# The four x tiles issued by ScalarE's queue at the start of a two-layer encoder kernel

## The chip, the core and the metric

The kernel runs on one core of one Trainium2 chip. The metric is the device time of one execution in microseconds (us). The engines are TensorE (PE, with PEld for its weight loads), VectorE (DVE), ScalarE (ACT), GpSimd (POOL) and SyncE (SP), which only issues DMAs here.

## The reference

x is 512 x 1024, float32. There are two layers. Each computes a modulation from the vector c, normalises x, projects it through a wide `w_in`, runs three token mixers, gates them and projects back:

```python
c_act = jax.nn.silu(c)
for l in range(DEPTH):
    mod = c_act @ w_ada[l] + b_ada[l]
    shift, scale, gate = [m[:, None, :] for m in split_cols(mod, (D, D, D))]
    h = rms_norm(x, g_pre[l]) * (1.0 + scale) + shift
    (cq, ckv, kr, za, qb_, kb_, vb_, zb, qc, kc, vc, zc, gcols) = split_cols(h @ w_in[l], IN_SPLITS)
    o_a = (mla_branch(cq, ckv, kr, ...) * jax.nn.silu(za)) @ w_o_mla[l]
    o_b = (swa_branch(qb_, kb_, vb_, ...) * jax.nn.silu(zb)) @ w_o_swa[l]
    o_c = (diff_branch(qc, kc, vc, ...) * jax.nn.silu(zc)) @ w_o_diff[l]
    y = (g[:, :, 0] * o_a + g[:, :, 1] * o_b + g[:, :, 2] * o_c) @ w_out[l]
    x = x + gate * rms_norm(y, g_post[l])
```

## The kernel before

Every matrix product in full precision is made of three matmuls (`mm3`, L86 to L89): each operand is split into a rounded part, made by ACT (`act_copy`, L81), and a rest, made by DVE or POOL (`sub`, L84). Tokens lie in the free dimension, 512 wide; the model dimension is cut into eight tiles of 128, numbered j = 0 to 7 here.

The change lies in the first stage, `layer0_input` and what is written ahead of it. It does these things:

- c is loaded (L156) and put through its silu: a tanh on ACT (L180) and two small steps on DVE (L181, L182) make `cact`.
- The modulation's shift and scale for layer 0 are a product of `cact` and `w_ada`. `mod_load` (L143) loads column tiles of `w_ada` on SP's queue, `mod_chunk` (L187) multiplies them on DVE, one 128-row slice after the other (L203 for the first slice, L206 for the rest), adds up the partitions with tiny matmuls (L212) and leaves shift and scale in `ashf` and `amul` (L215, L217, L220). There are chunks for j = 0, for 1, for 2 and 3, for 4 and 5, and for 6 and 7. The tiles of chunk 0 are called wh and wl, later ones wh, wl and big.
- x is loaded in four token tiles of 128 x 1024 (`xt0`, called big, L165 and L166). `normed` (L322) takes each through a square and sum on ACT (L325), an addition on DVE (L318), a power on POOL (L319) and a scaling on DVE (L327). PE transposes the result (L346), ACT copies it out (L349 by way of L81).
- Then for each j ACT applies scale and shift (L363) and makes the rounded part of h (called hTh, L81), DVE the rest (hTl, L84). Two products follow on PE: the mixer's inputs (`mla_in_step`, weights called u and p, into ps_sc, ps_sc, ps_pj and ps_av, 416 columns) and three column tiles of z (weights loaded to tf, split into pt by ACT and POOL, into ps_dn, ps_dn and ps_tr, 512 columns; L369 to L371, nine matmuls for each j).
- The small parameters of `setup_small` come last: four loads for each lambda (L412), products and sums on DVE (L415, L417), an exponential on ACT (L418).
- After the stage ACT takes the statistics of the mixer's inputs (L612, L614), and the attention of the first mixer begins.

The code does not fix the order on an engine. A scheduler puts the instructions in order with a time model of its own, engine by engine; the order it leaves is static, and each engine works through its list. So an edit in one place can move instructions in others. A load signals its end on one of eight semaphores, which the loads of SP's and ACT's queues take in turn: a load waits until the one that had its semaphore eight loads earlier has landed. Buffers of one name are used in rotation.

Of the kernel before, what the change touches and what calls it, by code (L numbers as in the profile page):

```python
# [17 lines left out]
P = 128  # L18
# [3 lines left out]
NT = S // P  # L22
# [28 lines left out]
def hybrid_kernel(ctx, tc, x, c, w_ada, b_ada, g_pre, g_post, w_in, g_q, w_uq, g_kv, w_ukv,  # L51
# [6 lines left out]
    pe, act, dve, pool, sp = nc.tensor, nc.scalar, nc.vector, nc.gpsimd, nc.sync  # L58
# [4 lines left out]
    def T(tag, shape, dt=F32, bufs=None):  # L63
        count[0] += 1
        return sb.tile(shape, dt, tag=tag, name=f"{tag}_{count[0]}",
                       bufs=bufs or BUFS.get(tag, 1))
# [76 lines left out]
    def mod_load(l, j, n, tags):  # L143
        tags = iter(tags)
        res = []
        for which in range(2):
            raws = [T(next(tags), [P, KT // n, n * P]) for _ in range(n)]
            for i, raw in enumerate(raws):
                loads.append(sp.dma_start(out=raw, in_=w_ada[l].rearrange("(p k) b -> p k b", k=KT)
                             [:, i * (KT // n):(i + 1) * (KT // n),  # L150
                              which * D + j * P:which * D + (j + n) * P]))
            res.append([raws[k * n // KT][:, k % (KT // n)] for k in range(KT)])
        return res

    xt0 = [T("big", [P, D]) for _ in range(NT)]
    sp.dma_start(out=cT, in_=c.rearrange("b (p k) -> p (b k)", k=KT))  # L156
    src0 = mod_load(0, 0, 1, ("wh", "wl"))
    prm = [T("tf", [P, P]) for _ in range(2)]
# [2 lines left out]
    for k, src, n in ((PR_GQ, g_q, 2), (PR_GKV, g_kv, 1), (PR_GSUB, g_sub, 1)):  # L161
        pool.dma_start(out=prm[1][k - 32:k - 32 + n * DEPTH, :],
                       in_=src.rearrange("l (a b) -> (l a) b", b=P))
    pool.dma_start(out=prm[1][0:16, :], in_=b_ada[1, 0:2 * D].rearrange("(a b) -> a b", b=P))
    for t in range(NT):  # L165
        sp.dma_start(out=xt0[t], in_=x[t * P:(t + 1) * P, :])  # L166
    prT = []

    for i, n in enumerate((32, PR_ROWS - 32)):
# [1050 lines left out]
```

## Time and profile before

| | us |
|---|---|
| median of 3 runs | 1180.55 (1180.5 to 1180.76) |
| profiled execution | 1178.78 |
| span of its instructions | 1176.7 |
| PE busy | 1146.0 (97%) |
| DVE busy | 844.2 (72%) |
| ACT busy | 631.5 (54%) |
| POOL busy | 181.3 (15%) |

The span runs from the first to the last instruction of the profiled execution; its own time is 2.1 us more. Busy times are sums over the whole kernel, so what one stage is bound by has to be read from windows and from the timeline of that stage.

### The profile page before, as it was taken

How to read it: one execution, taken by the hardware profiler on the slowest of the kernel's cores; microseconds unless marked ns; L12 is line 12 of the kernel's file. 1: busy time of each engine (PE TensorE's matmuls, PEld its weight loads, DVE VectorE, ACT ScalarE, POOL GpSimd, SP SyncE). 2: the span in 40 equal slices, each digit the busy share in tenths (PEclk: the TensorE clock that was granted, in tenths of full speed). 3: DMA queues.
4: the chain of work that ended last, by engine and by line, in shares of the span. 5: the costliest groups of instructions: out<-in, count | busy, mean ns of one | idle time of the engine just before them, and what ended most of it. 6: DMA issues, size and time to landing. Idle time of an engine off the chain costs nothing.

```text
span 1176.7 us, 15536 instructions
## 1 busy us (share of the span) xinstructions
PE 1146.0 (97%) x5428; PEld 946.0 (80%) x5428; DVE 844.2 (72%) x1754; ACT 631.5 (54%) x1250; POOL 181.3 (15%) x226
## 2 busy tenths in 40 slices
PE   5899999999999999999999999999999999999997
PEld 4768788878887888888888888888888888888886
DVE  7956686898866687876577567688786568786654
ACT  5355464655543457664357456565564346675432
POOL 4310212122210010101211011222121001100120
PEclk9899999999999999999999999999999999999999
DMA  9537532256355433433454432324533333334442
GB/s 340 190 92 217 186 106 76 72 145 186 108 141 164 110 81 87 117 107 126 143 184 135 114 108 75 86 52 123 157 97 92 95 95 96 88 99 115 136 159 92
DMA packets 169522, 146.86 MB, mean 125 GB/s; under 512 B 7679, under 2 KB 146999, under 8 KB 169444
## 3 DMA queue, kind: packets, MB, share of 16 engines
q1 hardware_dynamic: 166148, 140.08, 40.9%
q10 hardware_dynamic: 3168, 5.77, 1.3%
q8 instruction: 43, 0.70, 0.2%
q14 instruction: 35, 0.29, 0.1%
q0 software_dynamic: 128, 0.01, 0.0%
HBM read 135.83 MB, written 14.20 MB: 127 GB/s over the span
## 4 chain that ended last, share of the span: by engine, by line
PE 84%; DVE 6%; DMA 3%; issue 3%; ACT 1%; POOL 1%; SPq 0%; DVEq 0%; POOLq 0%; ACTq 0%
PE ps_dn L87 20%; PE ps_dn L89 20%; PE ps_dn L88 19%; PE ps_tr L704 5%; PE ps_sc L89 2%; PE ps_sc L87 2%; PE ps_sc L88 2%; PE ps_av L714 1%; PE ps_av L713 1%; PE ps_sc L952 1%; PE ps_sc L953 1%; DMA wr<-in_w_in 1%; DVE o L206 1%; PE ps_pj L87 1%; PE ps_pj L88 1%
## 5 line engine op out<-in xcount | busy, mean ns | idle before, releaser
L87 PE MATMUL ps_dn<-hTh,wh 128*128 128x512 f32 x840 | 331.8, 395 | 1.4 <-DVE zz L479 0.8
L89 PE MATMUL ps_dn<-hTh,wl 128*128 128x512 f32 x840 | 330.5, 393 | 0.4 <-DVE wl L84 0.4
L88 PE MATMUL ps_dn<-hTl,wh 128*128 128x512 f32 x840 | 330.1, 393 | 0.0
L84 DVE TENSOR_TENSOR wl<-wr,wh 128x1024 fp32r<-128x1024 f32 x141 | 178.9, 1269 | 98.5 <-ACT wh L81 97.5
L81 ACT ACTIVATE wh<-wr 128x1024 fp32r<-128x1024 f32 x141 | 149.1, 1058 | 162.7 <-PE ps_dn L88 111.2
L87 PEld LDWEIGHTS ps_dn<-hTh,wh 128*128 128x128 f32 x840 | 158.2, 188 | 33.2 <-PE ps_dn L89 1.0
L89 PEld LDWEIGHTS ps_dn<-hTh,wl 128*128 128x128 f32 x840 | 158.0, 188 | 33.3 <-DVE wl L84 0.9
L88 PEld LDWEIGHTS ps_dn<-hTl,wh 128*128 128x128 f32 x840 | 158.1, 188 | 31.7
L84 DVE TENSOR_TENSOR pt<-ps_tr,pt 128x512 fp32r<-128x512 f32 x136 | 92.2, 684 | 30.5 <-ACT pt L81 29.6
L81 ACT ACTIVATE pt<-ps_tr 128x512 fp32r<-128x512 f32 x136 | 78.8, 596 | 64.8 <-PE ps_tr L704 63.6
L775 POOL TENSOR_SCALAR p<-p,st 128x512 f32<-128x512 f32 x64 | 52.2, 834 | 279.3 <-DVE st L773 243.7
L704 PE MATMUL ps_tr<-ident,p 128*128 128x128 f32 x544 | 92.4, 273 | 0.9 <-POOL p L775 0.6
L704 PEld LDWEIGHTS ps_tr<-ident,p 128*128 128x128 f32 x544 | 69.5, 141 | 20.2 <-POOL p L775 1.8
L87 PE MATMUL ps_dn<-u,wh 128*128 128x512 f32 x192 | 75.9, 395 | 0.0
L89 PE MATMUL ps_dn<-u,wl 128*128 128x512 f32 x192 | 75.9, 395 | 0.0
L88 PE MATMUL ps_dn<-u,wh 128*128 128x512 f32 x192 | 75.2, 391 | 0.0
L963 POOL TENSOR_SCALAR ta<-ta,st 128x512 f32<-128x512 f32 x32 | 26.7, 834 | 306.9 <-ACT wh L81 143.1
L894 POOL TENSOR_SCALAR p<-p,st 128x256 f32<-128x256 f32 (+1 forms) x64 | 42.1, 676 | 157.7 <-DVE st L892 130.4
L771 ACT ACTIVATE p<-ps_sc,st 128x512 f32<-128x512 f32 x64 | 43.7, 685 | 28.0 <-DVE st L770 27.7
L770 DVE TENSOR_REDUCE st<-ps_sc 128x1 f32<-128x512 f32 x64 | 43.4, 686 | 21.3 <-PE ps_sc L89 20.8
L886 ACT ACTIVATE p<-p,st 128x256 f32<-128x256 f32 (+1 forms) x64 | 35.7, 558 | 21.9 <-DVE st L884 21.2
L959 ACT ACTIVATE p<-p,st 128x512 f32<-128x512 f32 x32 | 23.1, 723 | 38.8 <-DVE st L957 38.7
(345 smaller groups left out, 2100.5 us busy)
## 6 DMA issues: line engine op xcount, KB each, us to landing
wr<-in_w_in SPq DMA_DIRECT2D x105, 512.0 KB, 3.7
wr<-in_w_ada SPq DMA_DIRECT2D x32, 512.0 KB, 3.6
wr<-in_w_out SPq DMA_DIRECT2D x16, 512.0 KB, 3.6
big<-in_w_ada SPq DMA_DIRECT2D x10, 512.0 KB, 7.6
big<-in_x SPq DMA_DIRECT2D x8, 512.0 KB, 5.3
wr<-in_w_o_mla SPq DMA_DIRECT2D x8, 512.0 KB, 4.0
wr<-in_w_o_swa SPq DMA_DIRECT2D x8, 512.0 KB, 3.4
wr<-in_w_o_diff SPq DMA_DIRECT2D x8, 512.0 KB, 3.7
```

The costliest lines, as they stand in the source:

```text
L81: return act.activation(out=out_, in_=in_, func=AF.Copy, scale=scale)
L84: return (eng or dve).tensor_tensor(out=out_, in0=a, in1=b, op=ALU.subtract)
L87: pe.matmul(o, ah, bh, start=start, stop=False)
L88: pe.matmul(o, ah, bl, start=False, stop=False)
L89: pe.matmul(o, al, bh, start=False, stop=stop)
L704: pe.transpose(tr[:, i * P:(i + 1) * P], b, ident)
L770: dve.tensor_reduce(out=nm[:, t:t + 1], in_=s, axis=AX.X, op=ALU.max, negate=True)
L771: act.activation(out=pr[:, t], in_=s, func=AF.Exp, bias=nm[:, t:t + 1], accum_out=sm[:, t:t + 1])
L775: pool.tensor_scalar(out=pr[:, t], in0=pr[:, t], scalar1=rr[:, t:t + 1], scalar2=1.0, op0=ALU.mult, op1=ALU.mult)
L886: act.activation(out=pr[:, i, :w], in_=pr[:, i, :w], func=AF.Exp, bias=nm[:, i:i + 1], accum_out=sm[:, i:i + 1])
L894: pool.tensor_scalar(out=pr[:, i, :w], in0=pr[:, i, :w], scalar1=rr[:, i:i + 1], scalar2=1.0, op0=ALU.mult, op1=ALU.mult)
L963: pool.tensor_scalar(out=pc[1], in0=pc[1], scalar1=rr[:, 1:2], scalar2=1.0, op0=ALU.mult, op1=ALU.mult)
```

## The change

The four loads of x are written ahead of the load of c, and are issued by ACT (`act`) instead of SP.

```diff
     xt0 = [T("big", [P, D]) for _ in range(NT)]
+    for t in range(NT):
+        act.dma_start(out=xt0[t], in_=x[t * P:(t + 1) * P, :])
     sp.dma_start(out=cT, in_=c.rearrange("b (p k) -> p (b k)", k=KT))
     src0 = mod_load(0, 0, 1, ("wh", "wl"))
     prm = [T("tf", [P, P]) for _ in range(2)]
...
     pool.dma_start(out=prm[1][0:16, :], in_=b_ada[1, 0:2 * D].rearrange("(a b) -> a b", b=P))
-    for t in range(NT):
-        sp.dma_start(out=xt0[t], in_=x[t * P:(t + 1) * P, :])
     prT = []
```

The order of the instructions moves in the first stage alone. Three places of it follow. In the names, the number at the end tells buffers of one kind apart; the line numbers of the changed kernel are two higher from L156 to L166.

SP's list at its beginning, after the change, with the semaphores waited for (DMAHW0 to 7 are those of the loads):

```order
L158 DMA cT_65<-in_c 128x8
L149 DMA wh_94<-in_w_ada 128x8x128
L149 DMA wl_96<-in_w_ada 128x8x128
L161 DMA tf_98<-in_b_ada 16x128
L162 DMA tf_98<-in_g_pre 16x128 [waits DMAHW0_49]
L584 DMA wr_240<-in_w_in 128x2x416 [waits DMAHW1_49]
L149 DMA wh_255<-in_w_ada 128x8x128 [waits DMAHW2_49]
L149 DMA wl_257<-in_w_ada 128x8x128 [waits DMAHW3_49]
```

DMAHW0 is the first x tile's, DMAHW2 that of wh_94: g_pre now waits for x, and the w_ada tile of j = 1 waits for that of j = 0. Before, the four x loads stood between g_pre and wr_240, and neither waited so.

DVE's list after the two steps of `cact`, first part of the difference (wh and wl are the weights of chunk 0, big_146 and so on the normalised token tiles):

```order
+L203 TENSOR_SCALAR o_123<-wh_94,cact_66 128x128
+L206 SCALAR_TENSOR_TENSOR o_123<-wh_94,cact_66,o_123 128x128
+L318 TENSOR_SCALAR st_149<-st_147 128x1
+L206 SCALAR_TENSOR_TENSOR o_123<-wh_94,cact_66,o_123 128x128 x4
+L327 TENSOR_SCALAR big_146<-big_85,st_150 128x1024
+L206 SCALAR_TENSOR_TENSOR o_123<-wh_94,cact_66,o_123 128x128
+L318 TENSOR_SCALAR st_157<-st_155 128x1
+L203 TENSOR_SCALAR o_124<-wl_96,cact_66 128x128
+L206 SCALAR_TENSOR_TENSOR o_123<-wh_94,cact_66,o_123 128x128
+L206 SCALAR_TENSOR_TENSOR o_124<-wl_96,cact_66,o_124 128x128
+L327 TENSOR_SCALAR big_154<-big_86,st_158 128x1024
```

Before, all sixteen multiplies of wh and wl came first, and then the four scalings L327 one after the other with the additions L318 between them. Now the normalisation of the token tiles stands between the multiplies. The list still begins with wh.

ACT's list around the scale and shift of j = 4 and 5 (op_222 and op_223; pt_442 is the z weight of j = 3, pt_378 that of j = 2, wh_681 the weight of a later column tile of z):

```order
 L81 ACTIVATE x_149_694<-ta_691,prT_25_112 128x128
-L81 ACTIVATE pt_442<-tf_441 128x384
+L81 ACTIVATE pt_378<-tf_377 128x384
 L363 ACTIVATE op_222<-op_222,ashf_7_69,amul_5_67 128x512
 L363 ACTIVATE op_223<-op_223,ashf_7_69,amul_5_67 128x512
+L81 ACTIVATE wh_681<-wr_680 128x1024
+L81 ACTIVATE pt_442<-tf_441 128x384
 L81 ACTIVATE hTh_120<-op_222 128x512
 L81 ACTIVATE hTh_120<-op_223 128x512
-L81 ACTIVATE wh_681<-wr_680 128x1024
+L81 ACTIVATE wh_858<-wr_857,prT_25_112 128x512
```

The splits of z's weights stand one j later in ACT's list, and two copies stand between L363 and hTh. PE's list has the z matmuls of j = 3 ahead of the first that reads hTh of j = 4, before and after. POOL's list has pt_443, the rest that goes with pt_442, at the same place as before.

## Rows read from the trace of the kernel before

**Rows 1.** The page's part 2: busy tenths of PE in 40 slices of the span.
```profile
PE   5899999999999999999999999999999999999997
```

**Rows 2.** Windows: stretch and its length in us, busy us (instructions) by engine, PEclk, DMA, GB/s.
```profile
0.00:5.00 5.00, 0.00 (x0) 0.00 (x0) 0.83 (x8) 1.49 (x2) 2.98 (x10) 1.00 0.46 130
5.00:10.00 5.00, 0.28 (x1) 0.18 (x1) 3.71 (x14) 1.07 (x2) 0.00 (x0) 1.00 1.07 382
...
5.40:17.40 12.00, 5.43 (x24) 4.28 (x24) 8.98 (x26) 5.92 (x11) 3.88 (x6) 1.00 1.08 381
17.40:50.40 33.00, 28.40 (x135) 24.85 (x134) 32.32 (x74) 14.65 (x31) 13.74 (x11) 0.84 0.87 299
```

**Rows 3.** Timeline, SP and ACT at the start: start us, us, engine, line, operation [idle before, releaser].
```profile
0.73 1.28 ACT L180 ACT_TABLE_LOAD   x1 [0.73 <-PEq L1200]
1.17 0.67 SPq L149 DMA_DIRECT2D wh<-in_w_ada  x1
2.49 0.21 ACT L180 ACTIVATE st<-cT 128x8 f32<-128x8 f32 x1 [0.48 <-DMA cT<-in_c]
4.25 1.84 SPq L166 DMA_DIRECT2D big<-in_x  x4
```

**Rows 4.** Timeline, DVE: its first weight multiply, multiplies beside POOL, and the scale of j = 4, 5.
```profile
5.42 0.29 DVE L203 TENSOR_SCALAR o<-wh,cact 128x128 f32<-128x128 f32 x1 [2.32 <-DMA wh<-in_w_ada]
...
43.28 1.75 DVE L206 SCALAR_TENSOR_TENSOR o<-big,cact,o 128x256 f32<-128x256 f32 x2
44.55 1.01 DVE L206 SCALAR_TENSOR_TENSOR o<-big,cact,o 128x256 f32<-128x256 f32 x2
50.44 0.16 DVE L220 TENSOR_TENSOR amul<-amul,prT 128x2 f32<-128x2 f32 x1
50.52 2.85 DVE L206 SCALAR_TENSOR_TENSOR o<-big,cact,o 128x256 f32<-128x256 f32 x7
```

**Rows 5.** Timeline, ACT around the scale and shift of j = 4 and 5.
```profile
42.09 0.51 ACT L81 ACTIVATE pt<-tf 128x384 fp32r<-128x384 f32 x1
...
50.64 1.52 ACT L363 ACTIVATE op<-op,ashf,amul 128x512 f32<-128x512 f32 x2 [8.04 <-DVE amul L220]
52.07 1.13 ACT L81 ACTIVATE hTh<-op 128x512 fp32r<-128x512 f32 x2
53.11 1.04 ACT L81 ACTIVATE wh<-wr 128x1024 fp32r<-128x1024 f32 x1
54.06 0.51 ACT L81 ACTIVATE pt<-tf 128x384 fp32r<-128x384 f32 x1
```

**Rows 6.** Timeline, PE's restart, its last nine z matmuls (first, last), and ACT at the end.
```profile
52.73 0.46 PE L87 MATMUL ps_sc<-u,hTh 128*128 128x416 f32 x1 [2.94 <-ACT hTh L81]
...
68.08 0.35 PE L89 MATMUL ps_sc<-u,hTl 128*128 128x416 f32 x1
...
68.74 0.20 ACT L418 ACTIVATE st<-st 128x2 f32<-128x2 f32 x1 [2.11 <-DVE st L417]
68.85 0.37 ACT L612 ACTIVATE ta<-ps_sc 128x256 f32<-128x256 f32 x1
...
69.39 0.39 PE L87 MATMUL ps_dn<-hTh,pt 128*128 128x512 f32 x1
...
71.20 0.39 PE L89 MATMUL ps_tr<-hTh,pt 128*128 128x512 f32 x1
```

**Rows 7.** Windows and PE's timeline: the still stretches of PE, and matmuls at low clock.
```profile
31.90:34.20 2.30, 0.00 (x0) 0.00 (x0) 2.16 (x6) 0.00 (x0) 0.00 (x0) 1.00 1.04 369
34.30:41.10 6.80, 6.80 (x19) 5.59 (x20) 6.69 (x17) 4.60 (x11) 2.23 (x2) 0.50 1.03 331
...
49.80:52.70 2.90, 0.00 (x0) 0.00 (x0) 2.87 (x12) 2.06 (x4) 0.00 (x0) 1.00 0.00 0
...
36.08 0.63 PE L87 MATMUL ps_dn<-hTh,pt 128*128 128x512 f32 x1
36.51 0.63 PE L88 MATMUL ps_dn<-hTl,pt 128*128 128x512 f32 x1
```

## The prediction, made before the changed kernel had run

> **What bounds the kernel now.** Read the busy digits first [rows 1]: TensorE (PE) shows 9 in nearly every one of the 40 slices, so from the third slice on the kernel is a line of matmuls, and a delay or a gain of the first 70 us goes through to the end one for one. The change touches only that first stage, so I read the stage, in windows [rows 2]. The DMA engines are full from 5 us on (share 1.07, 382 GB/s) and only half used before (0.46, 130 GB/s). VectorE (DVE) is the bound next: from 5.4 to 17.4 us it is busy 8.98 of 12.0 us, from 17.4 to 50.4 us 32.32 of 33.0. DVE starts at 5.42 us, when the first modulation weight tile wh lands [rows 4], and it ends this chain at 50.44 us with the scale of columns 4 and 5 (L220). ScalarE (ACT) has waited 8.04 us for that value [rows 5], and PE has waited 2.94 us for what ACT makes of it [rows 6]. From 52.73 us PE runs without a break to the stage's end at 71.4. So two things decide: when DVE reaches that L220, and how much PE work stands behind it.
>
> **The change part by part.**
>
> The issues themselves. Four x issues leave SP (1.84 us together) and go to ACT's queue [rows 3]. ACT's order now has them ahead of the table load (1.28 us) and the tanh, which ran at 2.49. By the same 0.46 us each, the tanh comes at about 0.73 + 1.84 + 1.28 = 3.9 us. Its product is wanted at 5.42, so this costs nothing; without that cover it would cost the 1.4 us. SP's next weight loads do not move up by the same 1.84 us: in the order after, g_pre waits for the first x tile and the next w_ada tile waits for wh itself, since the load's semaphore is used again.
>
> When wh lands. Nothing in this trace has two full hardware queues side by side, so I bound it. If x does not disturb wh, DVE starts at 5.42 as now. If all of x goes first, wh is later by 4 x 0.524 MB / 381 GB/s = 5.5 us. (Below the first bound there is nothing: wh is issued at the same place of SP's queue.) I take the middle, **+2.75 us**: x's first tiles are issued with or before wh, but x's four tiles cannot all be in before wh's first bytes are under way. The windows tell why it must cost something: the engines are full as soon as both queues run, so the new queue brings work forward only in the half empty first 5 us. The Trainium skill, "DMA: Bandwidth & Descriptors", section "Issuing engines are not separate DMA queues", says as much: transfers issued by different engines run on the same 16 DMA engines and interleave, and a second issuer saves only issue time. By an even interleaving wh's 1.4 us of bytes would take twice as long, the delay would be about 1.4 us and the sum below 0.4 instead of 1.75; no run so far shows which it is.
>
> DVE's idle time. Between 5.4 and 17.4 DVE idles 12.0 - 8.98 = 3.02 us [rows 2], waiting in turn for weights and for the statistics of x. In the new order the four row normalisations (L318, L327) stand between the weight multiplies, with x landed before, so the waits on GpSimd's power are covered by multiplies. I leave 0.5 us for the rest: **-2.5 us**.
>
> DVE's list up to L220 of columns 4 and 5. One 128x256 multiply of columns 6 and 7 fewer stands ahead of it: seven of them take 2.85 us [rows 4], so **-0.4 us**. One GpSimd subtract (L84 for z's fourth row tile) also moves behind it. Two DVE multiplies took 1.75 us beside that subtract and 1.01 after it [rows 4]: **-0.75 us**.
>
> So L220 comes at 50.44 + 2.75 - 2.5 - 0.4 - 0.75 = 49.5 us, 0.9 us earlier.
>
> Behind L220 the scheduler has made ACT's queue worse. Before, the split pt_442 ran at 42.09, while ACT was waiting anyway, and after the two L363 came the two hTh [rows 5]. Now wh_681 and pt_442 stand between L363 and hTh. From the start of L363 it was 52.73 - 50.64 = 2.09 us to PE's next matmul. Now it is 1.43 (52.07 - 50.64) for two L363, 0.95 (54.06 - 53.11) for wh_681, 0.51 for pt_442 and 0.05 to start: 2.94 us. **+0.85 us**. Queued behind them are hTh, on which PE and DVE wait.
>
> What PE finds there. Before, the nine z matmuls of row tile 3 (they read pt_442) ran ahead of the wait. Now pt_442 comes after it, so these nine join the unbroken stretch. Nine such matmuls take 9 x (71.20 - 69.39)/8 = **+2.05 us** [rows 6]. Nothing in the later list shrinks for it: the other row tiles' matmuls are the same.
>
> The stage's end. ACT's L612 started at 68.85 though its matmul, the last of ps_sc, started at 68.08 with 0.35 us: it stood behind the exponential of the lambda at 68.74 [rows 6]. The lambda loads wait for GpSimd's subtracts, not for PE, and with PE later they are early: **-0.3 us**.
>
> Sum: -0.9 + 0.85 + 2.05 - 0.3 = **+1.7 us**. The profiled execution took 1178.78 us (span 1176.7 and 2.1 around it), so it would be 1180.5; the runs' median, 1180.55, is 1.8 above the profiled execution, and the forecast on that scale is **1182.3 us**. Differences below 0.2% (2.4 us) cannot be told from no change here, so this is "same", near the edge. With wh's two bounds the sum runs from -1.05 to +4.5.
>
> **The rivals.**
>
> (a) PE's clock falls in the longer wait: slower. Before, PE stood still from 49.8 to 52.7 and the clock stayed at 1.00; after the still stretch of 31.9 to 34.2 it was 0.50 for 6.8 us, that is 1.2 of 2.4 GHz [rows 7]. What PE did around the two differs, so the rows leave it open. Now the nine matmuls (2.05 us) go from the front of the wait to its back and the wait ends 0.85 later: it grows from 2.94 to about 5 us, since L220 is earlier by about as much as what stands before the wait. At half clock a matmul starts every 0.43 us (36.08 to 36.51) instead of 0.23. Each 3 us of it in the unbroken stretch lose 1.4, the 6.8 us seen before would lose 3.2. It decides from about 1 us of low clock after the restart on. Time: 1.7 + 1.4 to 3.2, about 1184.5. For it: a wait well above the one that did cost the clock. Against it: the first still stretch followed sparse work, this one dense work.
>
> (b) wh is late by nearly all of x, without (a). DVE starts near 10 us; L220 falls 1 to 2 us behind its old time; sum +3 to +4.5, about 1184.3. For it: x's rows are 4 KB and the w_ada tile's 512 B, so turn by turn x would get most of the bytes. Against it: x's issues are spread over 1.84 us and wh's comes after the first. The Trainium skill, "DMA: Bandwidth & Descriptors", section "Queues, rings and completion order", says that a DMA engine goes round between the queues that have work, packet by packet; whether such a packet is one row of a tile no run so far shows.
>
> (c) wh hardly late: the idle time of DVE is won nearly whole. Sum -1 to 0, and if DVE also loses less beside GpSimd, -2.5. About 1179.8. Against it: full DMA engines from 5 us on.
>
> (d) The change does nothing: x arrives early, but DVE's order still begins with wh, and other slack in the stage (z's loads on SP wait for GpSimd anyway) takes up both gain and loss. 1180.5.
>
> **How the numbers follow.** Chances: the forecast 0.45 (its own range +0.3 to +3.2, some 0.1 of it above 2.4), (a) 0.24, (b) 0.11, (c) 0.14, (d) 0.06. Slower by over 0.2%: 0.10 from the forecast, 0.19 from (a), 0.09 from (b): 0.38. Faster by over 0.2%: 0.08, nearly all from (c), where the price of DVE beside GpSimd is open. Same: 0.54. The range leaves out the far ends of (a), (b) and (c): 1179.0 to 1185.3.
>
> **What the profile after would show.** DVE's first L203 between 6.8 and 9.5 us rather than 5.42; DVE's idle time between there and 17.4 below 1 us; L220 of columns 4 and 5 between 48.5 and 50.5; ACT's L363, wh, pt, hTh in this row; nine z matmuls at the head of PE's unbroken stretch, which ends 1 to 3 us later than 71.4. The granted clock between 50 and 60 us settles (a). I am wrong if the unbroken stretch does not start with z, if L203 starts at 5.4 or after 10, or if something after 75 us changes.

## The result, and the profile after

The changed kernel took **1185.02 us** (median of five runs, 1183.51 to 1186.23) against 1180.55 (1180.34 to 1180.77): ratio 1.0038, 95% interval 1.0023 to 1.0052, so 4.5 us slower. The forecast was 1182.3, its range 1179.0 to 1185.3; the time lies in it, near the upper end, where rival (b) stood (1184.3). The profiled execution took 1184.74 us, its span 1182.7.

x did arrive early, and the first weights paid for it. SP's and ACT's start, against [rows 3]:

```profile
0.73 1.86 ACTq L157 DMA_DIRECT2D big<-in_x  x4
1.18 0.68 SPq L149 DMA_DIRECT2D wh<-in_w_ada  x1
2.61 4.25 SPq L161 DMA_DIRECT2D tf<-in_b_ada  x1
2.62 1.28 ACT L180 ACT_TABLE_LOAD   x1 [2.62 <-issue]
4.19 0.21 ACT L180 ACTIVATE st<-cT 128x8 f32<-128x8 f32 x1 [0.29 <-DMA cT<-in_c]
10.11 0.55 SPq L149 DMA_DIRECT2D wh<-in_w_ada  x1
```

The four issues take 1.86 us and push the table load and the tanh back, to 4.19 us, where nothing waits for them. wh is issued at the same time as before. SP's own next issue, of only 8 KB, then takes 4.25 us, and the load of the next wh, which waits for the first one to land, comes at 10.11. The windows (stretch and its length, busy us and instructions by engine, PEclk, DMA share, GB/s) answer to [rows 2]:

```profile
0.00:5.00 5.00, 0.00 (x0) 0.00 (x0) 0.83 (x8) 1.73 (x3) 2.98 (x10) 1.00 0.48 182
5.00:10.00 5.00, 0.00 (x0) 0.00 (x0) 0.00 (x0) 3.92 (x7) 0.00 (x0) 1.00 1.07 382
10.20:22.20 12.00, 6.44 (x26) 4.79 (x26) 11.05 (x32) 2.07 (x6) 4.59 (x6) 1.00 1.10 371
22.20:52.00 29.80, 27.34 (x122) 25.19 (x122) 28.76 (x67) 13.80 (x30) 11.29 (x9) 0.94 0.77 258
```

From 5 to 10 us DVE and PE do nothing at all, and ACT squares x, which nobody can use yet. The DMA engines move little more in the first 5 us (182 GB/s, 130 before: 0.26 MB) and are full after them, as before: the second queue brought little forward and mainly changed who is served first. The trace's rows by queue say who that was (q10 is ACT's queue, on which x alone lies, q1 is SP's; pieces moved, MB, share of the engines' time), first from 0 to 5 us, then from 5 to 8 us:

```profile
q10 hardware_dynamic: 237, 0.91, 46.2%
q1 hardware_dynamic: 144, 0.00, 1.4%
```
```profile
q10 hardware_dynamic: 269, 0.97, 79.1%
q1 hardware_dynamic: 426, 0.22, 24.0%
```

In the first 5 us no weight moves, though wh is issued at 1.18; SP's 144 pieces there fit c, whose 128 rows of 32 B stand ahead of wh. In the next 3 us x gets more than four times the weights' bytes. DVE's first weight multiply and its scale of columns 4 and 5, against [rows 4]:

```profile
10.19 0.29 DVE L203 TENSOR_SCALAR o<-wh,cact 128x128 f32<-128x128 f32 x1 [5.38 <-DMA wh<-in_w_ada]
...
51.99 0.14 DVE L220 TENSOR_TENSOR amul<-amul,prT 128x2 f32<-128x2 f32 x1
```

DVE starts 4.77 us later and reaches the scale 1.55 later. ACT and PE behind it, against [rows 5, 6]:

```profile
52.17 1.52 ACT L363 ACTIVATE op<-op,ashf,amul 128x512 f32<-128x512 f32 x2 [5.37 <-DVE amul L220]
53.59 1.04 ACT L81 ACTIVATE wh<-wr 128x1024 fp32r<-128x1024 f32 x1
54.54 0.51 ACT L81 ACTIVATE pt<-tf 128x384 fp32r<-128x384 f32 x1
54.95 1.14 ACT L81 ACTIVATE hTh<-op 128x512 fp32r<-128x512 f32 x2
...
55.10 0.50 PE L87 MATMUL ps_dn<-hTh,pt 128*128 128x512 f32 x1 [2.54 <-ACT pt L81]
...
72.73 0.20 ACT L418 ACTIVATE st<-st 128x2 f32<-128x2 f32 x1 [3.34 <-DVE st L417]
72.84 0.37 ACT L612 ACTIVATE ta<-ps_sc 128x256 f32<-128x256 f32 x1
...
75.10 0.40 PE L89 MATMUL ps_tr<-hTh,pt 128*128 128x512 f32 x1
77.18 0.50 PE L87 MATMUL ps_dn<-hTh,wh 128*128 128x512 f32 x1 [0.78 <-DVE zz L479]
```

The split of wh and that of pt stand between the two scales and hTh, PE restarts with the z matmuls 2.93 us behind the first scale (2.09 before), and the last z matmul is 3.90 us later than in [rows 6]. The next stage's first matmul (the last line) was at 73.18 before: **4.00 us** later. All of the stage's loss is there, and later stages add to it: by the end of the trace the span is 6.0 us longer. Since e11 and e12 also lie some 1 us further from the profiled execution of before at their end than at 75 us, and that one was 1.8 us under its median, I take the growth for no effect of the change, which no run settles; the medians differ by 4.47.

### The profile page after: what moved, and what is told of

The parts are those of the page before. It is cut to its first block, busy times and chain, and to the rows that moved or that the text cites. A ratio compares the mean times of both kernels' runs of the same rounds, so it can differ in the third digit from the quotient of the medians.

```text
span 1182.7 us, 15535 instructions
## 1 busy us (share of the span) xinstructions
PE 1148.7 (97%) x5428; PEld 948.6 (80%) x5428; DVE 844.3 (71%) x1754; ACT 631.6 (53%) x1250; POOL 181.1 (15%) x226
## 4 chain that ended last, share of the span: by engine, by line
PE 80%; DVE 9%; DMA 6%; issue 2%; ACT 2%; POOL 1%; SPq 0%; DVEq 0%; POOLq 0%; ACTq 0%
PE ps_dn L87 19%; PE ps_dn L88 18%; PE ps_dn L89 18%; PE ps_tr L704 5%; DVE o L206 2%; DMA wr<-in_w_ada 2%; DMA wr<-in_w_in 2%; PE ps_sc L89 2%; PE ps_sc L87 2%; PE ps_sc L88 2%; PE ps_av L714 1%; PE ps_av L713 1%; PE ps_sc L952 1%; PE ps_sc L953 1%; DVE wl L84 1%
```

## The experiments

All kernels below ran beside runs of before on the same chip; those varied more there than in the first five (19 runs beside e1 to e4: 1178.05 to 1181.53, median 1179.36), so ratios are compared. Times in the table are us from the span's start in each kernel's trace; "spacing" is that of 128x416 matmuls right behind PE's restart, or of the 128x512 ones where z comes first; e4 and e8 have no stop there, and theirs is that at about 54 us.

| kernel | first weight multiply | scale of 4, 5 | PE restarts | spacing | next stage | ratio (95%) |
|---|---|---|---|---|---|---|
| before | 5.42 | 50.44 | 52.73 | 0.19 | 73.18 | 1 |
| change | 10.19 | 51.99 | 55.10 | 0.23 (z) | 77.18 | 1.0038 (1.0023 to 1.0052) |
| e1 | 10.13 | 52.68 | 56.14 | 0.35 | 77.23 | 1.0038 (1.0025 to 1.0050) |
| e2 | 5.39, wl 11.92 | 55.59 | 57.75 | 0.23 (z) | 79.50 | 1.0051 (1.0037 to 1.0064) |
| e3 | 6.48 | 50.33 | 53.40 | 0.35 | 75.53 | 1.0009 (1.0000 to 1.0018) |
| e4 | 9.96 | 51.41 | no stop | 0.19 | 76.97 | 1.0031 (1.0022 to 1.0041) |
| e5 | 10.08 | 52.60 | 54.88 | 0.19 | 79.62 | 1.0166 (1.0152 to 1.0179) |
| e8 | 5.26 | 50.10 | no stop | 0.19 | 76.69 | 1.0028 (1.0017 to 1.0038) |
| e9 | 10.15 | 52.86 | 55.14 | 0.19, then 0.35 | 77.76 | 1.0038 (1.0025 to 1.0050) |
| e10 | 5.28 | 50.80 | 53.09 | 0.19 | 72.74 | 0.9994 (0.9985 to 1.0003) |
| e11 | 10.10 | 52.66 | 54.92 | 0.35 | 75.73 | 1.0034 (1.0022 to 1.0047) |
| e12 | 6.43 | 49.63 | 51.90 | 0.19, then 0.35 | 72.56 | 0.9997 (0.9988 to 1.0006) |

**What is ahead of the weights: e2, e3, e4.** In e2 x is issued behind the tanh:

```diff
-    for t in range(NT):
-        act.dma_start(out=xt0[t], in_=x[t * P:(t + 1) * P, :])
...
-    act.activation(out=th, in_=cT, func=AF.Tanh, scale=0.5)
+    thi = act.activation(out=th, in_=cT, func=AF.Tanh, scale=0.5)
+    with behind(thi):
+        for t in range(NT):
+            act.dma_start(out=xt0[t], in_=x[t * P:(t + 1) * P, :])
```

> The four loads of x stay on ScalarE's queue but are issued behind its tanh, at about 2.7 to 4.5 us instead of 0.73 to 2.6. Theory A (the weights were late because x's tiles were ahead of them): the first weight multiply starts before 6.2 us; the multiplier of columns 4 and 5 comes between 49 and 50.5 us; here pt_442 stands between the two scales and hTh (+0.5) and six to nine z matmuls are in the unbroken stretch (+1.5 to 2.0), so about 1181.7 (1180.8 to 1182.8). Rival C (any second queue beside SyncE's delays the weights): the first weight multiply at 8 us or later, 1184 or more.

wh was on time, so theory A had that right; wl was not, and the kernel became the slowest of the three. DVE's and ACT's timelines of e2:

```profile
5.39 0.29 DVE L204 TENSOR_SCALAR o<-wh,cact 128x128 f32<-128x128 f32 x1 [2.43 <-DMA wh<-in_w_ada]
...
11.92 0.29 DVE L204 TENSOR_SCALAR o<-wl,cact 128x128 f32<-128x128 f32 x1 [5.09 <-DMA wl<-in_w_ada]
```
```profile
2.35 3.29 ACTq L181 DMA_DIRECT2D big<-in_x  x4
8.76 1.06 ACT L326 ACTIVATE big<-big 128x1024 f32<-128x1024 f32 x1 [6.20 <-DMA big<-in_x]
```

wl, issued at 1.89 us on SP, was overtaken by tiles of x issued from 2.35 us on: the first of them is in use at 8.76, wl at 11.92. Both my theories missed this: it is not enough to issue the weights first. In e3 only one tile of x is early:

```diff
-    for t in range(NT):
+    for t in range(1):
         act.dma_start(out=xt0[t], in_=x[t * P:(t + 1) * P, :])
...
+    for t in range(1, NT):
+        sp.dma_start(out=xt0[t], in_=x[t * P:(t + 1) * P, :])
```

> Only the first tile of x is issued by ScalarE at the beginning; the other three stay on SyncE's queue at their old place. Theory A (the weights wait for the tiles ahead of them): the first weight multiply is later by at most one tile, 1.4 us, so at 5.4 to 6.9 us; pt_442 is ahead of the scales here, wh_681 between them and hTh (+0.95): about 1181.5 (1180.5 to 1182.5). Rival C (a second queue costs by itself): 7 us or later, and 1183 or more.

The first multiply came 1.06 us later, as expected of one tile (theory A), and the ratio is between nothing and 1.0018. In e4 the four loads keep their new place in the program but go to SP's queue (act.dma_start becomes sp.dma_start in the line that the change added).

> x at the very beginning too, but on SyncE's own queue, ahead of c and of the weights: the order of the change without a second queue. Theory A (what counts is that x is ahead): the first weight multiply at 10 to 11 us as in the change; ScalarE's order at the wait is that of before, and four 128x256 multiplies fewer stand ahead of the multiplier of columns 4 and 5, so it comes at about 51 us: 1181.2 (1180 to 1182.5). Rival C (two queues side by side are the trouble): the weights land by 8 us.

9.96 us instead of 10.19 (wh, issued at 3.27 behind x and c, took 6.6 us to land), and a loss that cannot be told from the change's. So rival C falls: what makes the weights late is x ahead of them, on one queue or on two. The time itself I had wrong: 1.0031 is 1184.2 on the scale of 1180.55, above my 1182.5. PE did not stop at this scale at all; it ran at the granted clock of 0.50 on the way, by e4's window from 46.0 to 52.6 us:

```profile
46.00:52.60 6.60, 6.60 (x21) 6.01 (x21) 6.60 (x17) 3.68 (x7) 2.42 (x2) 0.50 0.12 33
```

So e4 shows what makes wh late, and not that its loss comes by the same path as the change's.

**How two queues share: e6, e7.** x in two transfers for each tile, with rows of 2 KB (e6) or in blocks of 512 B (e7):

```diff
+    def half(ap, h):
+        return ap.rearrange("p (two b) -> p two b", two=2)[:, h]
...
-        act.dma_start(out=xt0[t], in_=x[t * P:(t + 1) * P, :])
+        for h in range(2):
+            act.dma_start(out=half(xt0[t], h), in_=half(x[t * P:(t + 1) * P, :], h))
```

In e7 the rearrangement is "p (k two b) -> p two k b" with two=2, b=P.

> The change, with each tile of x loaded in two transfers: the left and the right half of the columns, so 128 rows of 2 KB each, eight issues on ScalarE's queue from 0.73 us to about 4.4. It is there for comparison with e7, which has the same eight issues and bytes in rows of 512 B. What is read is when the first weight tile is there (the first weight multiply on VectorE): turns row by row would let it land between the change's 10.1 us and e7's time; an order by issue alone puts it at the same time as in e7.

> As e6, but each of the two transfers of a tile takes every second block of 128 columns, so its pieces are 512 B, as long as the weights' own. Theory T (the two queues take turns piece by piece, so 4 KB against 512 B starved the weights): the first weight multiply starts at 6.5 to 8 us, at least 1 us earlier than in e6. Theory O (what counts is only how many bytes were issued ahead): the same as in e6 within 0.3 us.

The reading I had named was spoiled: ACT's eight issues stretch over 9.54 us in e6 and 10.34 in e7. A single one takes 0.33 to 0.45 us and 0.55 to 0.72; the later ones wait for the semaphores of earlier loads. So the tanh came at 11.60 and 12.40 and DVE began after it. But SP shows the landing, since its load of w_in (L588) waits for wh. SP's timeline in e6, then in e7:

```profile
1.17 0.67 SPq L149 DMA_DIRECT2D wh<-in_w_ada  x1
...
10.39 0.39 SPq L588 DMA_DIRECT2D wr<-in_w_in  x1
```
```profile
1.17 0.68 SPq L149 DMA_DIRECT2D wh<-in_w_ada  x1
...
6.31 0.39 SPq L588 DMA_DIRECT2D wr<-in_w_in  x1
```

Same bytes and the same eight issues, and wh is there 4.08 us earlier when x comes in pieces as short as wh's own. (At 6.31 us e7 had issued five of the eight and e6 six; the sixth is 0.26 MB, 0.7 us at 382 GB/s, so theory O falls all the same.) The rows by queue of e7 from 5 to 8 us:

```profile
q1 hardware_dynamic: 1044, 0.52, 58.2%
q10 hardware_dynamic: 859, 0.43, 48.0%
```

With equal pieces the two queues move about as many bytes; in the change, with 4 KB against 512 B, it was 0.97 MB against 0.22. So far theory T is borne out: the queue with the longer pieces takes the larger part of the bytes. The pieces did not go one for one, though (269 against 426 in the change), and e6 does not fit: I had expected wh between the change and e7, and it landed at 10.39 us, while in the change the load that waits for it is issued at 10.11. Rows of 2 KB helped nothing, although SP's queue in e6 had moved 0.69 MB by 8 us, more than the 0.52 of wh; why is open. As kernels the two are no use (single runs of 1185.78 and 1188.30 us, beside a median of before of 1177.91).

**What stands behind the wait: e1, e5, e11, e12.** All set ACT's order there back:

```diff
-            act_copy(zh[:, 0:ZK * P], zr)
+            zis.append(act_copy(zh[:, 0:ZK * P], zr))
...
-            act.activation(out=xT[j], in_=xT[j] if j else trs[0], func=AF.Identity,
-                           scale=amul[0][:, j:j + 1], bias=ashf[0][:, j:j + 1])
-            act_copy(hh[:, j], xT[j])
+            with behind(zis[3]) if j in (4, 5) else nullcontext():
+                act.activation(out=xT[j], in_=xT[j] if j else trs[0], func=AF.Identity,
+                               scale=amul[0][:, j:j + 1], bias=ashf[0][:, j:j + 1])
+            hi = act_copy(hh[:, j], xT[j])
+            if j == 5:
+                hth5.append(hi)
...
-            fence[:] = [amuls[-1]]
+            fence[:] = [amuls[-1], hth5[0]]
```

> x on ScalarE's queue as in the change; only ScalarE's order at the end of the wait is set back to the one of before: pt_442 ahead of the two scales of columns 4 and 5, and the split wh_681 behind the two hTh. Theory A (the terms add up: late weights, ScalarE's order, nine z matmuls behind the wait): the first weight multiply stays at about 10.2 us and the multiplier of columns 4 and 5 at about 52.0 us, but from the first of the two scales to TensorE's restart it is 2.1 us instead of 2.93, and the nine z matmuls of row tile 3 are back ahead of the wait: 0.85 and 1.5 to 2.0 us less, about 1182.4. Theory B (the late weights alone cost the 4.5 us, ScalarE's order is hidden by waits for GpSimd or loads): no difference to the change, about 1185.0.

No gain. In e1's timeline of ACT and PE, hTh begins 1.42 us behind the first scale, so ACT's part is repaired, but PE does not start on it:

```profile
52.87 1.52 ACT L366 ACTIVATE op<-op,ashf,amul 128x512 f32<-128x512 f32 x2 [5.71 <-DVE amul L221]
54.29 1.13 ACT L81 ACTIVATE hTh<-op 128x512 fp32r<-128x512 f32 x2
...
56.14 0.58 PE L213 MATMUL ps_tr<-ones,o 128*128 128x1 f32 x4 [1.73 <-DVE o L207]
56.58 0.61 PE L87 MATMUL ps_sc<-u,hTh 128*128 128x416 f32 x1
56.99 0.55 PE L88 MATMUL ps_sc<-p,hTh 128*128 128x416 f32 x1
57.33 0.55 PE L87 MATMUL ps_sc<-u,hTh 128*128 128x416 f32 x1
```

The scheduler had put column sums first, which wait for DVE, and behind them the matmuls are spaced 0.35 us instead of 0.19. The repair gave its gain back to a new wait and to the slow pace. It also moved GpSimd's subtract back ahead of the scale, which comes 0.69 us later than in the change: the term of 0.75, seen from the other side. e5 adds that PE's sums are written behind the matmuls of column 4 (mod_chunk split into steps, its PE part called behind mla_in_step, one step at j = 4 and one at j = 5).

> As e1 (x early on ScalarE's queue, ScalarE's order at the wait as before), and TensorE's order there is set back as well: in e1 TensorE's first matmuls behind the wait were the column sums of columns 6 and 7 (ones times o), which waited 1.73 us for VectorE, and the granted clock was 0.67 behind them. Here the eight matmuls on u_474 stand first again, as before. Theory A (the terms add up): the multiplier of columns 4 and 5 at about 52.7 us as in e1, TensorE restarts 2.1 us behind the first of the two scales, the clock stays at 1.00, and the stage ends 2.0 to 2.5 us later than before: ratio about 1.0019. Theory D (the clock falls whatever the order, since TensorE has nothing to do for 2 us or more): the clock is again below 1.00 between 55 and 60 us, and the loss stays at 3.5 us or more. Theory B (late weights alone cost the 4.5 us): ratio 1.0038 as the change.

The place in question went as theory A said (restart 2.09 us behind the scale at 52.79, spacing 0.19), but the second sum came too late, PE waited 4.20 us at 69 us for hTh of the last columns, and the order of later stages changed too. Its 1.0166 is therefore no verdict on the question. e11 calls both steps at j = 4 and leaves the later stages as they were.

> As e5, with the column sums of columns 6 and 7 kept close behind the matmuls on u_474 (in e5 the second of them came so late that TensorE waited 4.2 us at 66 us), and all that follows the stage in the order of the kernel before. Theory A (late weights, plus what stands behind the wait): the multiplier of columns 4 and 5 at about 52.6 us, TensorE's restart about 2.1 us behind the scale, then 0.19 us between matmuls; the next stage's first matmul at 75.2 to 75.9 us, against 77.18 in the change and 73.18 before; ratio 1.0017 to 1.0024. Theory D (a stop of 2 us or more brings the slow pace whatever the order): 0.35 us between the matmuls behind the restart, next stage at 76.5 or later, ratio 1.003 or more.

The restart is 2.09 us behind the scale (54.92 against 52.83) and the next stage begins at 75.73, both as theory A had them: setting the order back won 1.45 of the stage's 4.00 us, net of a scale 0.67 us later and of a slow pace. For theory D's slow pace is there too, in e11's PE timeline and windows:

```profile
54.92 0.59 PE L87 MATMUL ps_sc<-u,hTh 128*128 128x416 f32 x1 [2.02 <-ACT hTh L81]
55.31 0.55 PE L88 MATMUL ps_sc<-p,hTh 128*128 128x416 f32 x1
55.66 0.55 PE L87 MATMUL ps_sc<-u,hTh 128*128 128x416 f32 x1
```
```profile
50.00:55.00 5.00, 2.98 (x14) 2.14 (x12) 5.00 (x18) 2.17 (x4) 0.00 (x0) 1.00 0.22 69
55.00:60.00 5.00, 5.00 (x22) 4.90 (x23) 4.13 (x9) 2.78 (x5) 3.96 (x2) 0.66 0.09 23
```

By the whole time e11 cannot be told from the change; its ratio, 1.0034, lies in theory D's range and above theory A's. e12 is e3 with the edit of e1.

> As e3 (one tile of x early on ScalarE's queue), with wh_681 behind hTh and so the matmuls on u_474 ahead of the column sums of columns 6 and 7. In e3 TensorE stood still until 53.40, for those sums, and its matmuls behind were spaced 0.35 us. Theory A: the multiplier of columns 4 and 5 at 50.3 us as in e3, TensorE's restart at 52.4 to 52.6, 0.19 us between matmuls; next stage at 72.8 to 73.8 against 75.53 in e3 and 73.18 before: ratio 0.999 to 1.0005, and a version that is no slower than before. Theory D: slow pace behind the restart again, next stage at 74.5 or later, ratio as e3 (1.0009) or more.

The next stage begins 2.97 us earlier than in e3 and 0.6 earlier than before; the ratio, 0.9997, is that of no change, which theory A had; the slow pace came four matmuls behind the restart all the same. So one tile of x early, with the order behind the wait set back, neither costs nor gains anything that can be measured. e11 and e12 ran on one chip beside the same runs of before, both with the order set back: with four tiles early 1182.51 us, with one 1178.85. That is the clearest sight of what x ahead of the weights costs, some 3.7 us of whole time; the slow pace is in both.

**Whether another limit sits behind: e8, e9, e10.** e8 is the kernel before with the four normalisations (L327) on ACT instead of DVE (act_copy(xn, xt, rs[:, 0:1])).

> The kernel before (x on SyncE's queue), with the four row normalisations of the first stage moved from VectorE to ScalarE, which waits there. Theory V (VectorE's list decides when the multiplier of columns 4 and 5 is there): 0.75 x 3 + 1.54 us of work and three waits of 0.66 us leave VectorE, so the multiplier comes 2 to 5 us earlier than 50.44, and the kernel takes 1177 to 1179 (ratio 0.997 to 0.999). Theory W (the full DMA engines decide): VectorE waits for weights instead and the multiplier stays within 1 us of 50.44, the time within 0.1 per cent.

The scale came 0.34 us earlier, not 2 to 5, as W expected, but not for W's reason: what DVE waited for were ACT's squares, now behind ACT's own scalings. The ratio, 1.0028, lies in neither theory's range: in e8 PE waits 2.52 us until 65.42 for hTh of the last columns instead. From the waits of DVE in e8 (us in total, times, longest):

```profile
DVE st L318 <- ACT big L325: 4.2, 2, 2.2
DVE o L203 <- DMA wh<-in_w_ada: 2.3, 1, 2.3
DVE o L203 <- DMA wl<-in_w_ada: 1.0, 1, 1.0
```

e9 keeps PE busy early in the change (56 idle transposes ahead of the first tile of x, eight ahead of each other one):

```diff
         for t in range(NT):
+            for i in range(56 if t == 0 else 8):
+                pe.transpose(trs[0][:, t * P:(t + 1) * P], xn[t - 1][:, 0:P] if t else ident, ident)
             for j in range(KT):
```

> The change with idle transposes for TensorE: 56 transposes of the identity ahead of the first tile of x and eight more behind each tile's own (128x128, into a PSUM area that the next transposes overwrite). In the change's trace TensorE's matmuls were spaced 0.35 us from 28.6 to 33.0 us (0.19 from then on), and its transposes 0.21 at 22.8 (0.11 in the kernel before from 17.5 on). Theory P (the late, thin start left TensorE at the slow pace when the dense work began): with TensorE busy before, the matmuls on u and hTh from about 29 us on are spaced 0.19 from the beginning, 3 to 4.5 us of the slow pace go, and the kernel takes 1181 to 1183 on the scale of 1180.55 (ratio 1.000 to 1.002). Theory W (the end of the stage hangs on the weights alone, so TensorE only waits longer instead): the slow pace goes but waits on VectorE or ScalarE grow by as much; ratio 1.0035 or more.

Theory P was tested only in part. The dense work began at 27.75 us (29.03 in the change), but was at the slow pace again from 28.5 to 31.6. What lead there was, the z matmuls behind it at 31.60 instead of 33.34, was lost: PE waited 8.3 us in all from 20 to 60 us (6.1 in the change) and restarted at 55.14 (55.10). That fits theory W, by which PE only waits longer for DVE's chain. But the scale also came 0.87 us later than in the change and the order at the restart was another one, so e9 is not the change with a busy PE alone. e10 puts nine idle matmuls into before, ahead of the sums of columns 2 and 3:

```diff
+    fill = [0, None]
...
         stts.append(end)
+        for i in range(fill[0]):
+            pe.matmul(pst, fill[1][:, 0:P], fill[1], start=True, stop=True)
+        fill[0] = 0
...
+            if j == 2:
+                fill[:] = [9, hh[:, 1]]
```

> The kernel before, with nine idle matmuls (hTh by hTh, 128x512) ahead of the column sums of columns 2 and 3, where TensorE stood still from 31.9 to 34.2 us; behind that stop its matmuls were spaced 0.35 to 0.43 us until about 41 us. Theory P (the stop costs twice, by itself and by the slow pace behind it): without the stop the spacing behind it is 0.19 to 0.23, 2 to 3.5 us earlier at 41 us, and as far as VectorE's list allows the stage ends 0 to 3 us earlier: ratio 0.9975 to 1.000. Theory W (VectorE's list and the weights decide the stage's end): TensorE gains at 41 us and waits as much longer before 52.7; ratio 1.000 within 0.001.

The test failed: the idle matmuls ran at 38.75 us, behind the stop (PE still waited 1.87 us until 34.53), so the stop was not filled, and the ratio says nothing on theory P. In none of the twelve did a version beat the kernel before by more than its interval.

## Why the prediction was right or wrong

**The bound was right, the size was not.** The first 70 us decide, and the loss was made between DVE's first weight multiply and the next stage's first matmul, 4.00 of the 4.47 us. The time lies in the stated range only because that range takes in the rivals; the forecast's own, +0.3 to +3.2 us, does not reach +4.47.

**When wh lands: the mis-sized term.** I took the middle of 0 and 5.5, +2.75; it was +4.77, rival (b), which I gave 0.11. The step that failed is the one from "x's four tiles cannot all be in before wh's first bytes are under way" to the middle. The sentence itself held: of x's 2.10 MB 0.91 had moved by 5 us, when no weight had. But DVE needs wh's last bytes, and from 5 to 8 us x had 0.97 MB against 0.22, so nearly all of x was in first. e7 shows that x does not pass in this way when its pieces are as short as wh's, which was the reason that I had written for (b) and weighed too lightly; e6 shows that the length alone is not the whole of it. With 4.77 in place of 2.75 my sum is 1.7 + 2.0 = 3.7, against 4.0 in the stage. That it comes so near is in part luck, since the other misses nearly cancel: +0.8 for DVE's idle time, -0.35 for its list, -0.5 for z, +0.4 for the stage's end. The Trainium skill ("DMA: Bandwidth & Descriptors", "Issuing engines are not separate DMA queues") says that the transfers of several issuers interleave; that they do so evenly I had read into it. An even share, by the estimate in the prediction, gives a delay of 1.4 us; the change shows 4.77. The Trainium skill's rule of turns packet by packet ("DMA: Bandwidth & Descriptors", "Queues, rings and completion order") sets no share of bytes by itself: there a packet holds several descriptors, and no run here shows what a packet was.

**DVE's idle time.** Predicted -2.5 us. By [rows 2] DVE idled 3.02 + 0.68 = 3.70 us between its first multiply and the scale; in the change 0.95 + 1.04 = 1.99, so -1.7: less was won than I had put down.

**DVE's shorter list and the subtract.** Predicted -0.4 and -0.75. What is left of the scale's shift is 1.55 - 4.77 + 1.71 = -1.5 for both; e1 and e11, where the subtract is back, show 0.7 of it. I had stated 48.5 to 50.5 us for this scale, 49.5 in the sum; it came at 51.99, 2.0 us of that by the weights, 0.8 by DVE's idle time, less 0.35 by its list.

**ACT's order: right.** 2.94 us predicted, 2.93 measured, and 2.09 again in e5 and e11 where the order is set back.

**Nine z matmuls behind the wait.** Predicted +2.05. The nine did join the stretch, which begins 2.37 us later and ends 3.90 later, so it grew by 1.5. Part of the rest is that before it was not unbroken, as I had read it: PE waited 0.20 us at 64.67 for DVE's hTl, and does not in the change.

**The stage's end: not earned.** L612 again stands 0.11 us behind the exponential of lambda, as in [rows 6], so the -0.3 did not come: the lambda loads moved back with the rest.

**Rival (a)** did not happen in the change. PE stood still 2.54 us, less than before, because the z matmuls of column 2 ran late, and the window right behind shows the clock at 1.00:

```profile
55.00:60.00 5.00, 4.90 (x27) 4.50 (x28) 4.96 (x9) 2.64 (x6) 3.18 (x3) 1.00 0.16 39
```

It did happen in e1, e3, e9, e11 and e12, behind stops of 1.73 to 3.37 us, at the restart or a few matmuls later, while [rows 6] and the change restarted at full pace behind 2.94 and 2.54. So theory D, by the length of the stop alone, is no rule either. I was right to give (a) weight and had no rule for it; nor do I now.

**Rivals (c) and (d)** are excluded by the first weight multiply alone. My own condition (wrong if L203 starts after 10) was met, by 0.19 us, and the unbroken stretch ended 3.90 us later, where I had said 1 to 3.

## What to carry to other kernels

Where the DMA engines are already full, a second queue for data that is wanted later only changes who is served first: in e2 x, in 4 KB rows, overtook a weight tile in 512 B rows that had been issued before it, and in e7 x in 512 B pieces let the weights through 4.08 us earlier than in e6. Look at which queue's rows are longer before giving bulk data a queue of its own, and put the short-rowed critical load where nothing long can be beside it. And when a load moves, read the new order at the next big wait: here setting it back won 1.45 of 4.00 us in the stage (e11), which the whole times are too coarse to confirm, and repairing it on one engine alone (e1) gave nothing.

## What I had not expected

SP's issue of an 8 KB load, which waits for no semaphore, took 4.25 us (1.16 before): an issuing engine can be held at an issue, and with it all that stands behind on that engine. What held it the trace does not show. In e6 and e7 ACT, and the tanh behind its issues, were held for another reason, the semaphores that the loads take in turn.

PE's pace and the page's clock column do not always agree. In the change's PE timeline and windows:

```profile
29.87 0.55 PE L87 MATMUL ps_sc<-u,hTh 128*128 128x416 f32 x1
30.22 0.55 PE L88 MATMUL ps_sc<-p,hTh 128*128 128x416 f32 x1
...
44.13 0.55 PE L88 MATMUL ps_sc<-p,hTh 128*128 128x416 f32 x1
44.48 0.55 PE L87 MATMUL ps_pj<-u,hTh 128*128 128x416 f32 x1
```
```profile
28.00:33.00 5.00, 5.00 (x18) 4.82 (x19) 4.89 (x13) 1.99 (x4) 1.29 (x2) 1.00 1.08 388
44.00:46.00 2.00, 2.00 (x8) 1.90 (x7) 2.00 (x3) 2.00 (x8) 1.80 (x2) 0.50 0.36 123
```

At 30 us the same matmuls are spaced 0.35 us under a shown 1.00, as at 44 us under 0.50 (1.2 of 2.4 GHz). The trace's own list of granted clocks explains it: in the change it begins only at 33.33 us, and where it has no entry the column shows 1.00. From 33.34 us on the matmuls are at full pace (z's 0.23 us apart). Before, the list begins at 17.22 us, and the transposes go from 0.21 us apart to 0.11 there. So with the late start PE came to full pace 16 us later. What that costs by itself no run shows: before, the clock fell to 0.50 again from 24.05 to 27.46 and from 34.28 to 41.11 us, in the change only from 43.56 to 46.98, and until the scale DVE's chain decides. The spacing of like matmuls is the safer reading at the start of a trace; what decides the pace behind a stop stays open.
